# Recurrence gates as 64-row blocks, with both gates' weights side by side, in a hybrid encoder step on one core

## The chip, the core and the metric

The kernel runs on one NeuronCore of a Trainium2 chip. TensorE (PE) multiplies and PEld loads its weights; ScalarE (ACT), VectorE (DVE) and GpSimd (POOL) work beside it; SyncE (SP) issues most of the DMAs. Each engine executes its own instructions in order. The metric is the device time of one execution in microseconds (us), as a median of the runs shown.

## The reference, cut to what matters

One layer is computed for a prompt of 1024 frames and a sample of 64 frames, 1088 in all. An input projection gives, among others, the input `xa` of a recurrence with 1024 channels, a SiLU gate for it, and the operands of an attention branch. The recurrence has two sigmoid gates, `r` and `i`, whose weights are block diagonal: 16 blocks of 64 by 64.

```python
def rg_lru(u, h0, w_a, b_a, w_x, b_x, a_param):
    ub = u.reshape(B, L, N_BLOCKS_A, BLOCK_A)            # 16 blocks of 64 channels
    r = sigmoid(einsum('blnj,njk->blnk', ub, w_a).reshape(B, L, W_A) + b_a)
    i = sigmoid(einsum('blnj,njk->blnk', ub, w_x).reshape(B, L, W_A) + b_x)
    log_a = -LRU_C * r * softplus(-a_param)
    a = exp(log_a)
    x_in = sqrt(-expm1(2.0 * log_a)) * (i * u)
    # scan over time: h = a_t * h + x_t

ua, conv_new = causal_conv(xa, conv_hist, conv_w, conv_b)     # width 4
ya, h_new = rg_lru(ua, h0, w_rg_a, b_rg_a, w_rg_x, b_rg_x, a_param)
ya = ya * silu(ga)
```

The branch outputs are projected, gated, summed, projected again, normed and added to the input, and a last gated embedding is added.

## The kernel before, in words

Channels lie on partitions and time along the free dimension. The 1024 channels of the recurrence are eight groups of 128, `k` = 0 to 7, so that each group holds two of the 64-channel blocks. Every product of float32 operands is made of three matmuls: both operands are split in a high and a low part (`three`, L172 to L175, records the three lines for every such product).

The recurrence stands between the attention and the first output projection, in about 856 to 1042 us of the span. For each `k` it goes through these functions:

- `recur_in(k)` (L1456) fetches the gates' weights. It zeroes a 128x256 float32 tile `st` on POOL (L1466), and four DMAs put the four 64x64 blocks on the diagonals of its two 128x128 halves (L1471), one half for each gate. For `k` of 2 and more it returns the steps of the input projection panel of `xa`, whose three chunks of 364, 364 and 360 columns are copied out of PSUM into `xp` by ACT.
- `convolve(k)` (L1495) rounds the gate weights into `g_h` on ACT, makes the four taps of the convolution on DVE (L1501, L1504: tile `u`), and then the low part `g_l` on DVE.
- `split_u(k)` (L1509) splits `u` into `uh` (ACT) and `ul` (DVE).
- `gate(k)` (L1517) multiplies. For gate `i` (tile `x`), then for gate `r`, and for each of three chunks of 364 columns, three matmuls over 128 rows fill one bank of PSUM (`gacc`), and one ACT activation (L1526) writes 128x364 sigmoids. That makes 18 matmuls and 6 activations for each `k`.
- `mix_u`, `decay`, `decay_a`, `root`, `state_in`, `scan` and `output` (L1530 to L1586) make the recurrence on ACT and DVE: exponential, tanh and square root on ACT, the products and the scan on DVE.
- `own_gate(k)` (L1593) is the panel of the SiLU gate; its chunks are finished by ACT (L1598) and DVE (L1599). For `k` of 1, 3 and 5 it was made earlier and is only loaded; `early_gate` (L1608) finishes it.
- `split_y(k)` (L1588) splits the branch's output into `yah` and `yal`, the operands of the next projection.

Each panel's weights are loaded ahead (`look_ahead`), split by `split_next` (L284): ACT makes `wh` and a negated copy `wl`, and a DMA issued by POOL (L291) adds the raw weights onto `wl`.

The order of PE, ACT and DVE in this part is the order in which the program calls these functions (`manual_schedule`). For a pair of groups, `k` even and `k+1`, it is, on PE: gate(k), the SiLU panel of k, the input panel of k+2, gate(k+1), the input panel of k+3, and then gate(k+2). Of tiles with the suffix `_e` (odd `k`) and without it (even `k`) there is one buffer each, so that the activations of gate(k+2) write the `x` and `r` that group `k` has used. PSUM has eight banks for this part. After gate(6) PE makes the SiLU panel of 6, a third of one left-over gate panel (called f here), gate(7), the rest of f, the SiLU panel of 7 and then the first panels of the output projection (`Held`, tiles `held`), which need `yah` and `yal` one group after the other, group 7 last.

Of the kernel before, what the change touches and what calls it, by code (L numbers as in the profile page):

```python
# [8 lines left out]
F32 = mybir.dt.float32  # L9
F32R = mybir.dt.float32r  # L10
AF = mybir.ActivationFunctionType
# [3 lines left out]
P = 128  # L15
D = 1024
KT = D // P
# [6 lines left out]
HD = 64  # L24
# [13 lines left out]
W_SC = 1092  # L38
GC = 364
# [28 lines left out]
def hybrid_step(tc, a, o):  # L68
    nc = tc.nc
    PSUM = bass.MemoryType.PSUM  # L70
    act, dve, pool, pe, sp = nc.scalar, nc.vector, nc.gpsimd, nc.tensor, nc.sync

    def sb(name, bufs=1, side=None):
        kw = {"side": side} if side else {}
        return Pool(tc, name=name, bufs=bufs, reuse_waits="tile", **kw)

    def ps(name, bufs=1):
        return Pool(tc, name=name, bufs=bufs, space=PSUM, reuse_waits="tile")

    def f(ap):  # L80
        return ap.bitcast(F32)

    def copy_act(out, in_, scale=1.0):
        return act.activation(out=out, in_=in_, func=AF.Copy, scale=scale)  # L84

    def sub(eng, out, in0, in1):
        return eng.tensor_tensor(out=out, in0=in0, in1=in1, op=ALU.subtract)  # L87
# [43 lines left out]
    vt = cst.tile([P, 96], F32, name="vt")  # L131
# [4 lines left out]
    def tiny(n, name, w=1, tag=None):  # L136
        return small.tile([P, w], F32, name=name, tag=tag or name)[:n, :]
# [34 lines left out]
    def three(out, ah, al, bh, bl, start, stop):  # L172
        pe.matmul(out, ah, bh, start=start, stop=False)  # L173
        pe.matmul(out, ah, bl, start=False, stop=False)  # L174
        pe.matmul(out, al, bh, start=False, stop=stop)  # L175
# [16 lines left out]
    def panel_steps(pl, wh, wl, xs, evac, chunks=CH):  # L192

        for c, (t0, n) in enumerate(chunks):
            acc = pl.tile([P, 512], F32, name="acc", tag="acc")
            for k in range(KT):
                three(acc[:, :n], wh[:, k, :], wl[:, k, :], xs[k][0][:, t0:t0 + n], xs[k][1][:, t0:t0 + n],
                      k == 0, k == KT - 1)
                if k == KT - 1:
                    evac(c, t0, n, acc[:, :n])  # L200
                yield
# [15 lines left out]
    wpool = sb("wpool", bufs=2)  # L217
# [78 lines left out]
    def panel(eng=None, rooms=None, split=True):  # L296

        look_ahead()
        if not ahead:
            return None  # L300
        split_next(eng or dve)
        tag, _, w, *_ = ahead.popleft()
        look_ahead()
        if split:
            split_next(eng or dve, rooms)
        look_ahead()
        return tag, w
# [7 lines left out]
    mm = ps("mm", bufs=2)  # L315
# [204 lines left out]
    for name in ("conv_w", "conv_b", "b_rg_a", "b_rg_x", "a_param", "state_h", "state_conv"):  # L520
        n = a[name].shape[0]
        fetch(vec[at:at + n, :], a[name])
        at += n
    V_CW, V_CB, V_BA, V_BX, V_AP, V_H0, V_HIST = 0, 32, 40, 48, 56, 64, 72
# [67 lines left out]
    for b in range(2, NBLK + 1):  # L592
        _, n, t0 = x_src[b]
        for c, (_, w) in enumerate(VCH):
            acc = p1v.tile([P, 512], F32, name="vacc", tag="vacc")
# [700 lines left out]
    for u, (h, q2) in enumerate(units):  # L1296
        p = h // 2
# [129 lines left out]
    mm = ps("mm8", bufs=8)  # L1427
# [4 lines left out]
    def shared(n, dt, name):  # L1432
# [1 line left out]

    lent = {n: shared(n, F32, f"{n}_e") for n in ("sg", "q", "u", "e", "x", "r")}
    p3 = sb("p3")
    early = {"g": [p3.tile([P, 2, P], F32R, name=f"g_{x}") for x in "hl"], "u": p3.tile([P, W_SC], F32, name="u"),
             "uh": p3.tile([P, W_SC], F32R, name="uh"), "ul": p3.tile([P, W_SC], F32R, name="ul", tag="ul"),
             "sg": p3.tile([P, T], F32, name="sg")}
    xps, us, gws, sig, eq, states, silus, outs = {}, {}, {}, {}, {}, {}, {}, {}  # L1440
# [1 line left out]
    def cv(v, k):  # L1442
        return vt[:, v + k:v + k + 1]
# [3 lines left out]
    def room(name, k):  # L1447
        if k in lent_k:
            return lent[name][:, :]
        if name in early:  # L1450
            return early.pop(name)[:, :]
        return p3.tile([P, T if name == "sg" else W_SC], F32, name=name)[:, :]
# [3 lines left out]
    def recur_in(k):  # L1456

        if k < 2:
            xp = p3.tile([P, W_SC + 3], F32, name="xp")
            sp.dma_start(xp[:, 3:SEQ + 3], d_x[k][:, :SEQ])  # L1460
            ready_x.append(sp.dma_start(xp[:, SEQ + 6:SEQ + 6 + DEC], d_x[k][:, SEQ:T]))
            pool.memset(xp[:, 0:3], 0.0)
            pool.memset(xp[:, W_SC + 2:W_SC + 3], 0.0)
        raw = wpool.tile([P, GC], F32, name="st")[:, :2 * P].rearrange("p (i n) -> p i n", i=2)
        gh, gl = early.pop("g") if k == 0 else [p3.tile([P, 2, P], F32R, name=f"g_{x}") for x in "hl"]
        pool.memset(raw[:, :, :], 0.0)  # L1466
        for i, name in enumerate(("w_rg_a", "w_rg_x")):
            for j in range(2):
                js = slice(j * HD, (j + 1) * HD)
                with tc.issue_after(ready_x[0].ins) if k < 2 else nullcontext():  # L1470
                    sp.dma_start(raw[js, i, js], a[name][2 * k + j])  # L1471
        if k >= 2:
            xp = p3.tile([P, W_SC + 3], F32, name="xp")
            pool.memset(xp[:, 0:3], 0.0)
            pool.memset(xp[:, W_SC + 2:W_SC + 3], 0.0)
        hist = vt[:, V_HIST:V_HIST + 24].rearrange("p (j k) -> p j k", k=KT)
        pool.tensor_copy(xp[:, SEQ + 3:SEQ + 6], hist[:, :, k])

        xps[k] = xp, raw, gh, gl
        if k < 2:  # L1480
            return None

        def evac(c, t0, n, z):
            m = min(n, SEQ - t0)
            copy_act(xp[:, t0 + 3:t0 + 3 + m], z[:, :m])
            if m < n:
                copy_act(xp[:, SEQ + 6:SEQ + 6 + DEC], z[:, m:n])

        tag, w = panel()
        assert tag == ("x", k)  # L1490
        return panel_steps(mm, *w, xs, evac)
# [2 lines left out]

    def convolve(k):  # L1495
        xp, raw, gh, gl = xps.pop(k)
        copy_act(gh[:, :, :], raw[:, :, :])
        pool.tensor_copy(fin[:, 0:3, k], xp[:, SEQ:SEQ + 3])
        pool.tensor_copy(fin[:, 3:6, k], xp[:, W_SC - 1:W_SC + 2])
        u = room("u", k)  # L1500
        dve.tensor_scalar(out=u, in0=xp[:, 0:W_SC], scalar1=cv(V_CW, k), scalar2=cv(V_CB, k),  # L1501
                          op0=ALU.mult, op1=ALU.add)
        for tap in range(1, 4):
            dve.scalar_tensor_tensor(out=u, in0=xp[:, tap:tap + W_SC], scalar=cv(V_CW + tap * KT, k),  # L1504
                                     in1=u, op0=ALU.mult, op1=ALU.add)
        sub(dve, gl[:, :, :], raw[:, :, :], f(gh[:, :, :]))
        us[k], gws[k] = u, (gh, gl)

    def split_u(k):  # L1509
# [7 lines left out]
    def gate(k):  # L1517

        (u, uh, ul), (gh, gl) = us.pop(k), gws.pop(k)
        x, r = room("x", k), room("r", k)  # L1520
        for i, dst, bias in ((1, x, V_BX), (0, r, V_BA)):
            for c in range(3):
                cs_ = slice(c * GC, (c + 1) * GC)
                acc = mm.tile([P, 512], F32, name="gacc", tag="acc")
                three(acc[:, :GC], gh[:, i, :], gl[:, i, :], uh[:, cs_], ul[:, cs_], True, True)
                act.activation(out=dst[:, cs_], in_=acc[:, :GC], func=AF.Sigmoid, bias=cv(bias, k))  # L1526
        sig[k] = x, r
        mixed[k] = u

# [105 lines left out]
    seq.__enter__()  # L1635
    ga = own_gate(0)
    recur_in(0)
    convolve(0)
    recur_in(1)
    split_u(0)  # L1640
    for k in range(0, KT - 2, 2):
        ga = own_gate(k) if k else ga
        if k == 0:
            run(ga)
        gate(k)
        convolve(k + 1)
        mix_u(k)
        if k:
# [5 lines left out]
        if k:  # L1654
# [3 lines left out]
            run(ga)  # L1658
        own_gate(k + 1)
        xa = recur_in(k + 2)  # L1660
        chunk(xa)
        chunk(xa)
        if k:
            split_y(k - 1)
        run(xa)
        gate(k + 1)
        convolve(k + 2)
        mix_u(k + 1)
        decay(k)
# [14 lines left out]
    k = KT - 2  # L1684
    ga = own_gate(k)
    gate(k)
    convolve(k + 1)
    mix_u(k)
# [6 lines left out]
    tag, w = panel()  # L1695
# [71 lines left out]
    for of in range(KT):  # L1767
        g = g_ahead.popleft()
# [16 lines left out]
        else:  # L1785
            tag, w = panel()
# [93 lines left out]
    for of in range(KT):  # L1880
# [9 lines left out]
        tag, w = panel()  # L1890
# [277 lines left out]
    for k in range(2):  # L2168
        raw = p7.tile([P, D], F32, name="ple")
# [7 lines left out]
    mm = bank_pool  # L2177
# [60 lines left out]
    n = x_src[b][1]  # L2238
# [12 lines left out]
    ss, r = tiny(n, "ss"), tiny(n, "r_r")  # L2251
    dve.tensor_reduce(out=ss, in_=ss4[:n, :], axis=AX.X, op=ALU.add)
    rstd_of(ss, r, 1.0 / D)
    for i in range(2):
        c = slice(i * D // 2, (i + 1) * D // 2)
# [51 lines left out]
```

## Time and profile before

| what | value |
|---|---|
| median of 3 runs | 1441.27 us (1440.69 to 1442.69) |
| the profiled execution, its own time | 1439.48 us |
| its span, first to last instruction | 1437.7 us |
| mean granted clock of TensorE | 0.998 |
| PE busy | 1417.8 us, 99% of the span |
| DVE, ACT, POOL busy | 62%, 50%, 25% |

A row of the timeline gives the start in us, the time taken by the row's instructions together, the engine, the line, the operation, the tile that is written and those that are read, and the count. A bracket at the end tells how long the engine sat idle before it and what released it. Matmuls overlap, so that the distance between the starts of two is what one costs. A row of a group view ends with busy time, the mean of one in ns, and the idle time before.

### The profile page before, as it was taken

What the parts mean: (1) busy time and instruction counts of PE and PEld (TensorE: products, weight loads), DVE (VectorE), ACT (ScalarE), POOL (GpSimd) and SP (SyncE); (2) the same over time, 40 slices, a digit from 0 to 9 for tenths busy, and PEclk for the clock granted to TensorE, in tenths of its full rate; (3) what the DMA queues carried; (4) which work ended last, traced back from release to release, by engine and by line L of the source; (5) the groups of instructions that cost most, each with busy time, mean ns of one, the idle gap of its engine ahead of it and who ended that gap; (6) DMA issues with size and microseconds to landing.
All of it is one profiled execution on the core that took longest, in us unless ns stands there. A gap on an engine that the chain in (4) does not pass through costs nothing.

```text
span 1437.7 us, 24839 instructions
## 1 busy us (share of the span) xinstructions
PE 1417.8 (99%) x9217; PEld 1357.9 (94%) x9217; DVE 897.0 (62%) x1630; ACT 719.0 (50%) x1331; POOL 357.5 (25%) x514
## 2 busy tenths in 40 slices
PE   9999999999999999999999999999999999999997
PEld 8999999999999999999999999999999999888887
DVE  5564766564432666656666666898737574777654
ACT  5423544442213666656666657777535332665443
POOL 0013333233204545544554531321011000000001
PEclk9999999999999999999999999999999999999999
DMA  6767556864247655554474645564269773324211
GB/s 223 217 128 108 148 159 185 173 174 134 92 131 194 169 115 125 148 137 125 118 152 110 105 108 81 93 99 86 71 234 309 261 236 121 136 73 149 78 48 45
DMA packets 138917, 201.18 MB, mean 140 GB/s; under 512 B 24372, under 2 KB 98844, under 8 KB 137772
## 3 DMA queue, kind: packets, MB, share of 16 engines
q1 hardware_dynamic: 119436, 158.96, 43.5%
q0 software_dynamic: 8160, 23.25, 5.8%
q10 hardware_dynamic: 11200, 17.38, 3.3%
q8 instruction: 73, 1.20, 0.3%
q14 instruction: 48, 0.39, 0.1%
HBM read 131.60 MB, written 66.36 MB: 138 GB/s over the span
## 4 chain that ended last, share of the span: by engine, by line
PE 84%; DMA 5%; DVE 5%; ACT 3%; issue 2%; SPq 0%; DVEq 0%; ACTq 0%; POOL 0%; POOLq 0%
PE quad L820 17%; PE acc L173 11%; PE acc L175 11%; PE acc L174 11%; PE pv L1213 5%; PE q L1951 5%; PE tp L1192 4%; PE s L1171 2%; PE s L1170 2%; PE vacc L173 2%; PE vacc L174 2%; PE vacc L175 1%; DMA wl<-w_raw 1%; PE vacc L478 1%; DMA d_mix<-st_a 1%
## 5 line engine op out<-in xcount | busy, mean ns | idle before, releaser
L173 PE MATMUL acc<-xh,wh 128*128 128x364 f32 x720 | 238.1, 331 | 0.2 <-ACT st L84 0.2
L175 PE MATMUL acc<-xh,wl 128*128 128x364 f32 x720 | 235.7, 327 | 0.0
L174 PE MATMUL acc<-xl,wh 128*128 128x364 f32 x720 | 235.7, 327 | 0.0
L173 PEld LDWEIGHTS acc<-xh,wh 128*128 128x128 f32 x720 | 135.4, 188 | 1.4 <-ACT st L84 0.5
L174 PEld LDWEIGHTS acc<-xl,wh 128*128 128x128 f32 x720 | 135.3, 188 | 0.5
L175 PEld LDWEIGHTS acc<-xh,wl 128*128 128x128 f32 x720 | 135.1, 188 | 0.0
L87 DVE TENSOR_TENSOR wl<-w_raw,wh 128x1024 fp32r<-128x1024 f32 (+1 forms) x55 | 61.4, 1118 | 76.2 <-ACT wh L84 76.1
L84 ACT ACTIVATE wh<-w_raw 128x1024 fp32r<-128x1024 f32 (+1 forms) x66 | 63.4, 962 | 86.6 <-PE quad L820 34.9
L820 PE MATMUL quad<-xh,wh 128*128 128x272 f32 x416 | 87.4, 291 | 2.0 <-ACT p__3343 L84 2.0
L820 PE MATMUL quad<-xl,wh 128*128 128x272 f32 x416 | 86.1, 288 | 0.0
L820 PE MATMUL quad<-xh,wl 128*128 128x272 f32 x416 | 86.0, 288 | 0.0
L1158 POOL TENSOR_SCALAR pb<-pb,sm 128x896 f32<-128x896 f32 (+1 forms) x64 | 61.3, 957 | 88.4 <-DVE sm L1157 65.7
L87 DVE TENSOR_TENSOR tl<-tp,th 128x512 fp32r<-128x512 f32 x96 | 65.1, 685 | 27.7 <-ACT th L84 27.3
L84 ACT ACTIVATE th<-tp 128x512 fp32r<-128x512 f32 x96 | 56.7, 594 | 39.8 <-PE tp L1192 39.2
L1155 ACT ACTIVATE pb<-pb,nm 128x896 f32<-128x896 f32 (+1 forms) x64 | 63.1, 986 | 18.3 <-DVE nm L1152 14.5
L820 PEld LDWEIGHTS quad<-xh,wh 128*128 128x128 f32 x416 | 65.3, 188 | 2.5 <-ACT p__3343 L84 2.2
L1170 PE MATMUL s<-k,q 128*128 128x128 f32 (+1 forms) x192 | 66.9, 351 | 0.0
L1152 DVE CUSTOM_DVE_ANT_0 pb<-s,mask 128x896 f32<-128x896 f32 (+1 forms) x64 | 64.7, 1011 | 3.1 <-PE s L1171 3.1
L820 PEld LDWEIGHTS quad<-xh,wl 128*128 128x128 f32 x416 | 65.5, 188 | 0.0
L820 PEld LDWEIGHTS quad<-xl,wh 128*128 128x128 f32 x416 | 65.4, 188 | 0.0
L1171 PE MATMUL s<-k,q 68*128 68x128 f32 (+1 forms) x192 | 63.5, 348 | 0.8 <-DMA k<-d_k 0.8
L1192 PE MATMUL tp<-ident,pb 128*128 128x128 f32 x416 | 63.7, 273 | 0.0
(726 smaller groups left out, 4097.4 us busy)
## 6 DMA issues: line engine op xcount, KB each, us to landing
w_raw<-in_w_in SPq DMA_DIRECT2D x56, 256.0 KB
q<-d_q SPq DMA_DIRECT2D x48, 256.0 KB
k<-d_k SPq DMA_DIRECT2D x48, 256.0 KB
w_raw<-in_w_in SPq DMA_DIRECT2D x64, 128.0 KB
w_raw<-in_w_branch SPq DMA_DIRECT2D x32, 256.0 KB
wl<-w_raw POOLq DMA_DIRECT2D x11, 512.0 KB, 4.6
wraw<-in_w_in SPq DMA_DIRECT2D x20, 256.0 KB
d_k<-oh ACTq DMA_DIRECT2D x16, 272.0 KB
```

Source lines behind the costliest of these rows:

```text
L84: return act.activation(out=out, in_=in_, func=AF.Copy, scale=scale)
L87: return eng.tensor_tensor(out=out, in0=in0, in1=in1, op=ALU.subtract)
L173: pe.matmul(out, ah, bh, start=start, stop=False)
L174: pe.matmul(out, ah, bl, start=False, stop=False)
L175: pe.matmul(out, al, bh, start=False, stop=stop)
L820: pe.matmul(acc[:, c, :CW], l[:, k, :], r[:, k, c * CW:(c + 1) * CW], start=(first and k == 0 and p == 0), stop=(k == 3 and p == 2), skip_ ...
L1152: at = book("D", now[0] + HOP_PE, per(D_MAX, n), lambda: dve.tensor_tensor_reduce(out=pr[:, :n], in0=s[:, :n], in1=m, scale=-1.0, scalar=- ...
L1170: pe.matmul(s[:, c0:c0 + w], t["q1"][:, q0:q0 + P], t["k1"][:, c0:c0 + w], start=True, stop=False)
L1171: pe.matmul(s[:, c0:c0 + w], t["q2"][:HD + 4, q0:q0 + P], t["k2"][:HD + 4, c0:c0 + w], start=False, stop=True)
L1192: pe.transpose(tp[:, o0 + i * P:o0 + (i + 1) * P], pr[par][:, kb * P:(kb + 1) * P], ident[:, :])
L1213: return pe.matmul(pv[:, c0:256], v, x[:, half * 256 + c0:(half + 1) * 256], **kw)
L1951: pe.matmul(acc, l[:, k, :], r[:, k, :], start=(first and k == 0 and i == 0), stop=(k == 3 and i == 2), skip_group_check=not first)
```

## The change

Each 64-row block is multiplied on its own. The stationary operand of a block is 64 rows by 128 columns and holds both gates' weights side by side; the block in the lower 64 partitions (j = 0) has the `i` gate's weights in the first 64 columns and the `r` gate's in the last 64, the block in the upper 64 partitions (j = 1) the other way round. The two blocks have a bank of PSUM each, and their matmuls take turns. A bank then holds both gates of one block: one gate's on the partitions where it belongs, the `r` gate's on the other 64. So each bank is finished by two activations of 64 partitions, of which the one for `r` writes to the other half of the partitions. Its bias comes from a small tile `b_ra` in which the halves of the bias are exchanged.

The matmuls stay 18 for each `k`, each with 64 rows instead of 128; the activations become 12 of 64x364 instead of 6 of 128x364. Tiles `g_h`, `g_l` and the raw weights are 128 columns wide instead of 256, the memset of `st` goes, and the four DMAs of 64x64 stay.

```diff
+    b_ra = p3.tile([P, KT], F32, name="b_ra")
+    for j in range(2):
+        pool.tensor_copy(b_ra[(1 - j) * HD:(2 - j) * HD, :], vt[j * HD:(j + 1) * HD, V_BA:V_BA + KT])
-    early = {"g": [p3.tile([P, 2, P], F32R, name=f"g_{x}") for x in "hl"], ...
+    early = {"g": [p3.tile([P, P], F32R, name=f"g_{x}") for x in "hl"], ...
...
-        raw = wpool.tile([P, GC], F32, name="st")[:, :2 * P].rearrange("p (i n) -> p i n", i=2)
-        pool.memset(raw[:, :, :], 0.0)
+        raw = wpool.tile([P, GC], F32, name="st")[:, :P]
...
-                    sp.dma_start(raw[js, i, js], a[name][2 * k + j])
+                    c0 = HD * (i == j)
+                    sp.dma_start(raw[js, c0:c0 + HD], a[name][2 * k + j])
...
-        for i, dst, bias in ((1, x, V_BX), (0, r, V_BA)):
-            for c in range(3):
-                cs_ = slice(c * GC, (c + 1) * GC)
-                acc = mm.tile([P, 512], F32, name="gacc", tag="acc")
-                three(acc[:, :GC], gh[:, i, :], gl[:, i, :], uh[:, cs_], ul[:, cs_], True, True)
-                act.activation(out=dst[:, cs_], in_=acc[:, :GC], func=AF.Sigmoid, bias=cv(bias, k))
+        blocks = [slice(j * HD, (j + 1) * HD) for j in range(2)]
+        for c in range(3):
+            cs_ = slice(c * GC, (c + 1) * GC)
+            accs = [mm.tile([P, 512], F32, name="gacc", tag="acc") for _ in blocks]
+            for i, (g, v) in enumerate(((gh, uh), (gh, ul), (gl, uh))):
+                for js, acc in zip(blocks, accs):
+                    pe.matmul(acc[:, :GC], g[js, :], v[js, cs_], start=(i == 0), stop=(i == 2))
+            for js, other, acc in zip(blocks, blocks[::-1], accs):
+                act.activation(out=x[js, cs_], in_=acc[js, :GC], func=AF.Sigmoid, bias=vt[js, V_BX + k:V_BX + k + 1])
+                act.activation(out=r[js, cs_], in_=acc[other, :GC], func=AF.Sigmoid, bias=b_ra[other, k:k + 1])
```

More of the change, by code (lines that the diff above doesn't have):

```diff
@@ L1436, in hybrid_step @@
     p3 = sb("p3")
-    early = {"g": [p3.tile([P, 2, P], F32R, name=f"g_{x}") for x in "hl"], "u": p3.tile([P, W_SC], F32, name="u"),
+    b_ra = p3.tile([P, KT], F32, name="b_ra")
+    for j in range(2):
+        pool.tensor_copy(b_ra[(1 - j) * HD:(2 - j) * HD, :], vt[j * HD:(j + 1) * HD, V_BA:V_BA + KT])
+    early = {"g": [p3.tile([P, P], F32R, name=f"g_{x}") for x in "hl"], "u": p3.tile([P, W_SC], F32, name="u"),
              "uh": p3.tile([P, W_SC], F32R, name="uh"), "ul": p3.tile([P, W_SC], F32R, name="ul", tag="ul"),
@@ L1463, in recur_in @@
             pool.memset(xp[:, W_SC + 2:W_SC + 3], 0.0)
-        raw = wpool.tile([P, GC], F32, name="st")[:, :2 * P].rearrange("p (i n) -> p i n", i=2)
-        gh, gl = early.pop("g") if k == 0 else [p3.tile([P, 2, P], F32R, name=f"g_{x}") for x in "hl"]
-        pool.memset(raw[:, :, :], 0.0)
+        raw = wpool.tile([P, GC], F32, name="st")[:, :P]
+        gh, gl = early.pop("g") if k == 0 else [p3.tile([P, P], F32R, name=f"g_{x}") for x in "hl"]
         for i, name in enumerate(("w_rg_a", "w_rg_x")):
@@ L1496, in convolve @@
         xp, raw, gh, gl = xps.pop(k)
-        copy_act(gh[:, :, :], raw[:, :, :])
+        copy_act(gh[:, :], raw)
         pool.tensor_copy(fin[:, 0:3, k], xp[:, SEQ:SEQ + 3])
@@ L1505, in convolve @@
                                      in1=u, op0=ALU.mult, op1=ALU.add)
-        sub(dve, gl[:, :, :], raw[:, :, :], f(gh[:, :, :]))
+        sub(dve, gl[:, :], raw, f(gh[:, :]))
         us[k], gws[k] = u, (gh, gl)
```

## The prediction

> **What bounds the kernel now.** I read the page first, then the waits of PE around the recurrence, then the timelines of the engines there, ACT's beside DVE's.
>
> ```profile
> span 1437.7 us, 24839 instructions
> PE 1417.8 (99%) x9217; PEld 1357.9 (94%) x9217; DVE 897.0 (62%) x1630; ACT 719.0 (50%) x1331; POOL 357.5 (25%) x514
> ```
>
> ```profile
> PE pv L1213 <- DVE y L1239: 0.6, 1, 0.6
> PE pv L1213 <- DVE diag0l L87: 0.3, 1, 0.3
> PE held L173 <- DVE st_a L1774: 0.2, 1, 0.2
> PE acc L173 <- ACT st L84: 0.2, 1, 0.2
> ```
>
> PE is busy all the time. The four rows of the second view are all its waits between 830 and 1080 us: 1.3 us. By these alone the kernel is bound by PE and every matmul that goes is a gain. But a share of busy time doesn't say how far PE is from its next wait, so the next rows look at its order in the recurrence: the first matmul of gates 1, 2, 4, 6, of the left-over panel f, of gate 7, and of what follows it.
>
> ```profile
> 881.18 0.33 PE L173 MATMUL gacc<-uh,g_h 128*128 128x364 f32 x1
> ...
> 896.10 0.33 PE L173 MATMUL gacc<-uh,g_h 128*128 128x364 f32 x1
> ...
> 937.85 0.33 PE L173 MATMUL gacc<-uh,g_h 128*128 128x364 f32 x1
> ...
> 979.60 0.33 PE L173 MATMUL gacc<-uh,g_h 128*128 128x364 f32 x1
> ...
> 994.51 0.33 PE L173 MATMUL acc<-xh,wh 128*128 128x364 f32 x1
> ...
> 998.51 0.33 PE L173 MATMUL gacc<-uh,g_h 128*128 128x364 f32 x1
> ...
> 1001.84 0.43 PE L173 MATMUL acc<-xh,wh 128*128 128x364 f32 x1 [0.17 <-ACT st L84]
> ```
>
> From gate 2 to gate 4, and again from 4 to 6, PE needs 41.75 us: three panels of 72 matmuls and two gates of 18, which are 252, so 0.166 us each. Now ACT over the same pair of groups:
>
> ```profile
> 881.38 0.53 ACT L84 ACTIVATE xp<-acc 128x296 f32<-128x296 f32 x2 [3.53 <-PE acc L175]
> 881.88 1.57 ACT L1526 ACTIVATE x_e<-gacc,vt 128x364 f32<-128x364 f32 x3
> ...
> 884.85 0.41 ACT L84 ACTIVATE g_h<-st 128x256 fp32r<-128x256 f32 x1
> ...
> 903.00 1.47 ACT L1526 ACTIVATE x<-gacc,vt 128x364 f32<-128x364 f32 x3 [0.47 <-DVE e L1567]
> ...
> 913.27 0.47 ACT L1598 ACTIVATE sg<-acc 128x364 f32<-128x364 f32 x1 [5.12 <-DVE yal L87]
> ...
> 923.15 1.11 ACT L84 ACTIVATE yah<-r_e 128x1088 fp32r<-128x1088 f32 x1 [3.55 <-DVE r_e L1586]
> ...
> 924.56 1.48 ACT L1526 ACTIVATE x_e<-gacc,vt 128x364 f32<-128x364 f32 x3
> 925.90 1.50 ACT L1526 ACTIVATE r_e<-gacc,vt 128x364 f32<-128x364 f32 x3
> 927.24 0.46 ACT L84 ACTIVATE g_h<-st 128x256 fp32r<-128x256 f32 x1
> ...
> 938.89 1.12 ACT L1556 ACTIVATE r<-r 128x1092 f32<-128x1092 f32 x1
> ...
> 945.45 1.02 ACT L1526 ACTIVATE x<-gacc,vt 128x364 f32<-128x364 f32 x2 [0.47 <-DVE e L1567]
> ...
> 987.91 1.48 ACT L1526 ACTIVATE x<-gacc,vt 128x364 f32<-128x364 f32 x3 [0.48 <-DVE e L1567]
> ```
>
> The activations of gates 2, 4 and 6 start 42.45 and 42.46 us apart, each released by the scan of two groups before (L1567 on DVE), not by PE, whose gate 2 was under way at 896.10. So beside PE's round of 41.75 us there runs a second one of 42.45 us, on ACT and DVE alone: scan, DVE's work up to 923.15, ACT's from there without a pause to the square root at 938.89, DVE's again up to the next scan. PE is carried by the lead that it has. How large that still is, DVE shows where it makes the operand `ul` of gates 4, 6 and 7 (third, fifth and sixth row):
>
> ```profile
> 911.89 1.28 DVE L87 TENSOR_TENSOR yal<-sg,yah 128x1088 fp32r<-128x1088 f32 x1
> ...
> 924.29 1.29 DVE L87 TENSOR_TENSOR yal<-r_e,yah 128x1088 fp32r<-128x1088 f32 x1 [0.74 <-ACT yah L84]
> ...
> 934.55 1.30 DVE L87 TENSOR_TENSOR ul<-u,uh 128x1092 fp32r<-128x1092 f32 x1 [2.49 <-ACT uh L84]
> ...
> 940.04 1.30 DVE L1560 SCALAR_TENSOR_TENSOR r<-e,r 128x1092 f32<-128x1092 f32 x1
> ...
> 977.00 1.30 DVE L87 TENSOR_TENSOR ul<-u,uh 128x1092 fp32r<-128x1092 f32 x1 [2.49 <-ACT uh L84]
> ...
> 995.60 1.29 DVE L87 TENSOR_TENSOR ul<-u_e,uh 128x1092 fp32r<-128x1092 f32 x1
> ```
>
> `ul` of group 4 is there at 935.85 and PE takes it at 937.85: 2.0 us to spare. For group 6 it is 978.30 and 979.60: 1.3 us. For group 7, 996.89 and 998.51: 1.6 us. Whatever makes the ACT-DVE round longer reaches PE after that, and a faster PE only arrives earlier at the same wait. The weights are as close: the low part of a panel's weights is a DMA that POOL issues behind ACT's split and, for f, behind two copies that wait for the scan.
>
> ```profile
> 976.26 0.87 POOL L291 DMA_DIRECT2D wl<-w_raw  x1 [2.91 <-ACT wl L84]
> ...
> 989.19 0.90 POOL L291 DMA_DIRECT2D wl<-w_raw  x1
> ```
>
> ```profile
> wl<-w_raw POOLq DMA_DIRECT2D x11, 512.0 KB, 4.6
> ```
>
> With the 4.6 us of the DMA view (median from issue to landing), the panel after gate 6 has its weights at 980.9 and f at 993.8, 0.7 us before its first matmul at 994.51.
>
> **The matmuls.** Nothing in this trace has 64 rows in each half of the array by turns. The nearest rows are the scores, with 68 rows and with 128:
>
> ```profile
> L1170 PE MATMUL s<-k,q 128*128 128x512 f32 x96 | 40.0, 417 | 0.0
> ...
> L1171 PE MATMUL s<-k,q 68*128 68x512 f32 x96 | 38.1, 397 | 0.0
> ```
>
> Half the rows leave a matmul as long as before, so the gain depends on whether the two blocks run at once. If they do, a pair costs one step of 0.166 us and a gate 9 steps, 1.5 us less; if not, 18 steps and nothing saved. I take the former, since the two blocks share neither rows, operands nor a bank, and keep both ends: at most 12 us of PE over eight gates. The Trainium skill (TensorE: Matmul & The Clock Gate, Part 3, measured speedup) gives 3.07 times for four blocks of 32 rows; an estimate by it, at the same efficiency for two (1.54 times), is 1.05 us a gate, and no run here shows it yet.
>
> **The activations.** Six more for each group. What 64 partitions cost against 128, both from PSUM, 256 columns:
>
> ```profile
> L84 ACT ACTIVATE lo<-pv 64x256 f32<-64x256 f32 x64 | 24.4, 381 | 26.8 <-PE pv L1213 21.2 <-PE pv L1279 1.5 <-DVE ys L1285 1.4
> ...
> L84 ACT ACTIVATE st<-tpk 128x256 f32<-128x256 f32 x19 | 6.9, 378 | 6.8 <-DMA out_k_prompt<-st 6.8
> ```
>
> 381 against 378 ns: half the partitions save nothing, and `lo` even moves partitions as the new `r` does. Three sigmoids go from 924.56 to 925.90, 0.447 us each. Twelve take 5.36 us, six 2.68, so each gate costs ACT 2.68 us more. Over eight gates that is 21 us, but only those on the round count:
>
> - Even gates, at 903.00: ACT later waits 5.12 us for DVE. The added 2.68 us delay `yah`, which `yal` at 911.89 needs; ACT has it there about 0.9 us early even so. Nothing, unless the activations are 0.1 us longer than I take them.
> - Odd gates, at 924.56: ACT doesn't pause from there to the square root (ending at 940.01, just ahead of DVE's `r` at 940.04). All 2.68 us go into the round. Further, `r_e` is now written second, at 925.01, while DVE reads the old `r_e` in `yal` from 924.29 to 925.58: a wait of 0.6 us, behind which the other activations queue. The narrower `g_h` (0.46 us) gives back between nothing and half; I take 0.1. Sum 3.2 us for each of gates 3 and 5.
> - Gate 1: ACT waits for PE (3.53 us), so PE's gain counts. PE starts 1.5 us earlier, at 879.68; the first activation came 0.70 us after gate 1 began (three steps and 0.2), so now at 880.38, and twelve end at 885.74, where `g_h` started at 884.85. With the 0.1 back: 0.8 us later.
>
> So the round is 0.8 us late after gate 1, 4.0 after gate 3 and 7.2 after gate 5. Then PE: `ul` of group 6 is there at 985.5, gate 6 ends at 987.0; its panel's weights land at 988.1 and it needs 11.9 us (982.6 to 994.51), so it ends at 1000.0; the weights of f land at 993.8 + 7.2 = 1001.0; a third of f (4.0 us) ends at 1005.0, when `ul` of group 7 (1004.1) is there; gate 7 ends at 1006.5. Before, what follows started at 1001.84: 4.7 us later. All 12 us saved on PE are in front of these waits and are lost there, except 1.5 at gate 7, already counted.
>
> Edits at nothing: eight memsets fewer and two small copies more on POOL (busy 25%); the copies' cover is the first SiLU panel. DMAs stay as many and as large. From 1001.84 on PE's next tie to the round is `yal` of group 7:
>
> ```profile
> 1041.10 1.29 DVE L87 TENSOR_TENSOR yal<-r,yah 128x1088 fp32r<-128x1088 f32 x1
> ```
>
> ```profile
> 1049.81 0.34 PE L173 MATMUL held<-yah,wh 128*128 128x364 f32 x1
> ```
>
> There at 1042.39 and taken at 1049.81, it stays off the path with the round 7.2 and PE 4.7 us later, so the delay stays to the end. On the profiled execution's 1439.48 us this makes 1444.2; on the median of 1441.27, 1.8 above it, **1446.0 us**.
>
> **Rivals.**
> - *The two blocks don't overlap*, so that the change doesn't do what it says. Gate 1 then gives its first bank after six steps instead of three, at 882.38, and ACT is 2.8 us late after it; 9.2 after gate 5. Gate 6 from 987.5 to 990.5, its panel to 1002.4, weights of f at 1003.0, gate 7 from 1007.0 to 1010.0: 8.2 us, so 1449.5. For it: no row shows an overlap. Against: nothing shared.
> - *Faster: the activations of 64 partitions are short, so that the round doesn't grow.* By the sums above PE's delay is the round's delay less 2.5 us (7.2 against 4.7), and the round's delay is 36 times one activation (twelve after each of gates 1, 3 and 5) less 8.9 us. Break-even is at 0.32 us an activation. At half of 0.447, in proportion to the partitions, the round gains 0.9 us and PE 3.4: 1437.9. (With no round to wait for it would be the whole 12 us: 1429.3.) Against it: 381 and 378 ns.
> - *No change*: activations between, near 0.32 us, or an ACT pause that I have overlooked takes them up: 1441.3.
> - PE idles for over 4 us ahead of gates 4 and 6 in my forecast. The Trainium skill (TensorE: Matmul & The Clock Gate, Part 1) says that idling of some 3.4 us halves TensorE's clock until about as long a stretch of work has passed. By that rule, an estimate, the restart after the last such wait costs up to 1.7 us, and the time would be 1447.7. No wait here is that long, so the trace is silent.
>
> **How the numbers follow.** The forecast has 0.55, the halves in turn without overlap 0.20, the faster rival 0.12, no change 0.13. The forecast's own range is 1444.2 (0.40 us an activation) to 1447.8 (0.50), which are 36 times 0.05 us up or down. The range over the cases leaves out the faster rival and little above the serial one: 1441 to 1450. About 0.2%, 2.9 us, is what a measurement of this kernel can tell from no change. Slower by more holds the forecast and the serial case, 0.75; same 0.13; faster 0.12.
>
> **What would show it.** Right: matmuls of `gacc` starting in pairs a few ns apart; 96 activations of 64x364 about 0.45 us apart; the activations of gate 6 at about 995.1 instead of 987.91; new waits of PE for `ul` of groups 4 and 6; what follows gate 7 at about 1006.5; fewer us of PE busy, in a longer span. Wrong: PE without new waits in the recurrence, activations much under 0.4 us apart, or gate 6 on ACT no later than before.

## The result, and the profile after

The changed kernel takes **1455.69 us** (median of five runs, 1453.88 to 1457.43) against 1441.27: a ratio of 1.01, 95% interval 1.0087 to 1.0113. It is slower, by 14.4 us. Of five executions of the kernel before, four took 1440.18 to 1442.69 us and one, which no comparison here counts, 2315.88. The forecast had the sign and the mechanism; its 1446.0 is a third of the way, and the range ended at 1450. The profiled execution took 1453.88 us, 14.4 more than the one before.

The page of the changed kernel:

```profile
span 1452.0 us, 24893 instructions
PE 1416.9 (98%) x9217; PEld 1350.4 (93%) x9217; DVE 895.9 (62%) x1630; ACT 749.5 (52%) x1379; POOL 355.9 (25%) x508
```

PE has nearly the same busy time in a span that is 14.3 us longer. Counted over the recurrence alone (window; length, then busy time and instructions of PE, PEld, DVE, ACT and POOL, then granted clock of TensorE (1.00 is full speed), DMA share and rate), first before, then after:

```profile
860.00:1020.00 160.00, 159.83 (x964) 159.52 (x964) 128.36 (x133) 117.82 (x169) 30.77 (x63) 1.00 0.51 90
```

```profile
860.00:1035.00 175.00, 159.08 (x965) 152.29 (x964) 126.03 (x129) 145.36 (x214) 28.09 (x57) 0.96 0.46 82
```

The same matmuls take 15 us longer here. PE went from no pause to 16 us of pauses, and ACT has 27.5 us more to do, in 45 instructions more. PE's waits between 830 and 1080 us, which were 1.3 us in all, are now led by these:

```profile
PE gacc L1530 <- ACT uh L84: 7.5, 3, 3.3
PE acc L173 <- DVE sg L1606: 3.1, 2, 2.1
PE gacc L1530 <- DVE ul L87: 2.7, 3, 0.9
PE acc L173 <- ACT st L84: 1.3, 1, 1.3
```

The gates wait for both halves of `u`, which ACT and DVE make late in their round. **The matmuls** did what the change says. Gate 0 on PE after (before it took from 866.26 to 869.27):

```profile
866.63 0.44 PE L1530 MATMUL gacc<-uh,g_h 64*128 64x364 f32 x2
866.90 0.33 PE L1530 MATMUL gacc<-ul,g_h 64*128 64x364 f32 x2
867.07 0.33 PE L1530 MATMUL gacc<-uh,g_l 64*128 64x364 f32 x2
...
868.09 0.33 PE L1530 MATMUL gacc<-uh,g_l 64*128 64x364 f32 x2
868.35 0.44 PE L173 MATMUL acc<-xh,wh 128*128 128x364 f32 x1
```

Each row is a pair, one block in the upper rows and one in the lower. The pairs follow each other at 0.166 us, as single matmuls did: the two blocks run at once. Only the step into the short form (866.63 to 866.90) and the one out of it (868.09 to 868.35) are 0.1 us longer. A gate takes 1.72 us instead of 3.01.

**The activations** are another matter. Those of gate 3 on ACT, after:

```profile
928.80 0.55 ACT L1532 ACTIVATE x_e<-gacc,vt 64x364 f32<-64x364 f32 x1
929.85 0.56 ACT L1533 ACTIVATE r_e<-gacc,b_ra 64x364 f32<-64x364 f32 x1 [0.50 <-DVE yal L87]
930.44 0.56 ACT L1532 ACTIVATE x_e<-gacc,vt 64x364 f32<-64x364 f32 x1
931.01 0.56 ACT L1533 ACTIVATE r_e<-gacc,b_ra 64x364 f32<-64x364 f32 x1
...
935.60 0.56 ACT L1533 ACTIVATE r_e<-gacc,b_ra 64x364 f32<-64x364 f32 x1
936.19 0.31 ACT L84 ACTIVATE g_h<-st 128x128 fp32r<-128x128 f32 x1
```

From 929.85 to 936.19 eleven activations take 6.34 us: they start 0.576 us apart, as on the other gates, where the forecast had 0.447. One alone lasts no longer than before (the 128-partition ones have medians of 564 to 590 ns). What has gone is that one started before the last had ended. The predicted wait of `r_e` for the old `yal` is there, 0.50 us instead of 0.6.

How late the round is can be read at the first activation of each gate. Before, gates 2, 4, 6 and 7 started at 903.00, 945.45, 987.91 and 1004.95. After:

```profile
906.23 0.56 ACT L1532 ACTIVATE x<-gacc,vt 64x364 f32<-64x364 f32 x1 [0.47 <-DVE e L1574]
...
954.22 0.56 ACT L1532 ACTIVATE x<-gacc,vt 64x364 f32<-64x364 f32 x1 [0.47 <-DVE e L1574]
...
1002.19 0.56 ACT L1532 ACTIVATE x<-gacc,vt 64x364 f32<-64x364 f32 x1 [0.43 <-DVE e L1574]
...
1016.59 0.46 ACT L84 ACTIVATE st<-acc 128x364 f32<-128x364 f32 x1
...
1020.22 0.56 ACT L1532 ACTIVATE x_e<-gacc,vt 64x364 f32<-64x364 f32 x1 [1.64 <-DVE e_e L1574]
```

That is 3.23, 8.77, 14.28 and 15.27 us late. With the odd gates between them (924.56 became 928.80, 967.01 became 976.79) the delay grows by 3.23 us over gate 1, by 1.01 over gate 2, 4.53 over gate 3, 1.01 over gate 4, 4.50 over gate 5 and 0.99 over gate 6. PE's first matmul behind gate 7 moves from 1001.84 to 1017.10, 15.26 us, and the first `held` from 1021.84 to 1037.01, 15.17. From there to the end about 0.8 us come back; single executions scatter by more than that.

So gates 3 and 5 cost 4.5 us each instead of 3.2, gate 1 costs 3.2 instead of 0.8, and an even gate, forecast as covered, costs 1.0. Where that cover failed shows on DVE, in the rows of group 2. Before:

```profile
905.09 4.14 DVE L1504 SCALAR_TENSOR_TENSOR u_e<-xp,vt,u_e 128x1092 f32<-128x1092 f32 x3
909.15 0.42 DVE L87 TENSOR_TENSOR g_l<-st,g_h 128x256 fp32r<-128x256 f32 x1
```

After:

```profile
908.32 4.14 DVE L1507 SCALAR_TENSOR_TENSOR u_e<-xp,vt,u_e 128x1092 f32<-128x1092 f32 x3
913.51 0.29 DVE L87 TENSOR_TENSOR g_l<-st,g_h 128x128 fp32r<-128x128 f32 x1 [1.05 <-ACT g_h L84]
```

`g_l` needs `g_h`, which ACT makes behind the last activation. Before, `g_h` was there at 906.14 (905.69 and 0.45) and DVE came for it at 909.15, 3.0 us to spare. Twelve activations at 0.576 are 4.2 us longer than six at 0.447; with 0.14 back for the narrower `g_h`, the spare time is overdrawn by 1.1 us, and DVE waits 1.05. The forecast looked one step too far on, at `yah` for `yal`.

### The profile page after: what moved, and what is told of

It reads as the page before. It is cut to its first block, busy times and chain, and to the rows that moved or that the text cites. A ratio compares the mean times of both kernels' runs of the same rounds, so it can differ in the third digit from the quotient of the medians.

```text
span 1452.0 us, 24893 instructions
## 1 busy us (share of the span) xinstructions
PE 1416.9 (98%) x9217; PEld 1350.4 (93%) x9217; DVE 895.9 (62%) x1630; ACT 749.5 (52%) x1379; POOL 355.9 (25%) x508
## 4 chain that ended last, share of the span: by engine, by line
PE 84%; DMA 5%; DVE 5%; ACT 4%; issue 2%; SPq 0%; POOL 0%; DVEq 0%; ACTq 0%; POOLq 0%
PE quad L820 17%; PE acc L173 11%; PE acc L175 11%; PE acc L174 11%; PE pv L1213 5%; PE tp L1192 4%; PE q L1958 4%; PE s L1171 2%; PE s L1170 2%; PE vacc L173 2%; PE vacc L174 1%; PE vacc L175 1%; PE vacc L478 1%; DMA d_mix<-st_a 1%; DMA d_q<-ko 1%
```

## Experiments

The theory after the result: the time goes into ACT's round, and what was mis-sized is the pace of the activations, with 0.13 us more for each. Its rivals: the 64-row matmuls themselves cost something; PE's own time counts, so that any saving there must show; the pace comes from the 64 partitions as such, or from writing to other partitions than are read; and TensorE's clock, which falls in the new waits, is part of the bill.

**1. New matmuls, six activations.** In the changed kernel each bank is finished by one activation over all 128 partitions, as before.

```diff
-            for js, other, acc in zip(blocks, blocks[::-1], accs):
-                act.activation(out=x[js, cs_], in_=acc[js, :GC], ...)
-                act.activation(out=r[js, cs_], in_=acc[other, :GC], ...)
+            for dst, v, acc in zip((x, r), (V_BX, V_BA), accs):
+                act.activation(out=dst[:, cs_], in_=acc[:, :GC], func=AF.Sigmoid, bias=cv(v, k))
```

> The changed kernel's 64-row matmuls, but each bank of PSUM is finished by one activation of 128 partitions, six for each group as in the kernel before. The gates come out wrong: half of each activation takes the other gate's values. Theory A (the twelve activations lengthen the ACT-DVE round, and TensorE's gain can't be had because it waits for the round): activations 0.45 us apart, no long wait of PE, and about 1438.5 us, so 3 us under the kernel before (1441.3) and far less than the 10 us that eight gates of 1.72 instead of 3.01 us save on PE. Theory B (the 64-row matmuls themselves, or the exchange between the array's two ways of working, cost the time): 1450 us or more. Theory C (nothing but PE counts): 1431.

Measured: 1440.7 us, ratio to before 1.0005 (0.9995 to 1.0015). No change: the 64-row matmuls cost nothing, and PE's shorter gates bring nothing either. Gate 3 on ACT:

```profile
923.49 0.57 ACT L1532 ACTIVATE x_e<-gacc,vt 128x364 f32<-128x364 f32 x1
924.60 0.57 ACT L1532 ACTIVATE r_e<-gacc,vt 128x364 f32<-128x364 f32 x1 [0.55 <-DVE yal L87]
925.06 0.56 ACT L1532 ACTIVATE x_e<-gacc,vt 128x364 f32<-128x364 f32 x1
925.51 0.56 ACT L1532 ACTIVATE r_e<-gacc,vt 128x364 f32<-128x364 f32 x1
```

The pace is 0.45 us again. I had expected about 3 us of gain. The round did start earlier (gate 2 at 902.06, 0.94 us; gate 3 at 923.49, 1.07 us), but in the new order `r_e` is written second and waits 0.55 us for `yal`; the same at gate 5. At gate 6 there are 0.13 us left. On PE the saving has turned into pauses:

```profile
860.00:1020.00 160.00, 154.12 (x969) 147.62 (x968) 128.06 (x133) 116.77 (x169) 34.44 (x57) 1.00 0.51 90
```

It idles 5.9 us of 160 where it had idled 0.2.

**2. Old matmuls, twelve activations.** The counterpart: 18 matmuls of 128 rows as before, and the twelve activations in the changed kernel's order. The edit is shown against the changed kernel; the wide weight tiles of the kernel before are back too.

```diff
-            for i, (g, v) in enumerate(((gh, uh), (gh, ul), (gl, uh))):
-                for js, acc in zip(blocks, accs):
-                    pe.matmul(acc[:, :GC], g[js, :], v[js, cs_], ...)
+            for i, acc in zip((1, 0), accs):
+                three(acc[:, :GC], gh[:, i, :], gl[:, i, :], uh[:, cs_], ul[:, cs_], True, True)
```

> The kernel before's 128-row matmuls, but finished by the twelve activations of 64 partitions of the changed kernel, in their order. The r gate is wrong: its halves are taken from the other half's channels. Theory A: the round is as long as in the changed kernel, gate 1's first activation is 1.1 us later (it waits for six steps of PE) and gate 7 takes 1.3 us longer: about 1458 us. Theory B (the matmuls cost the time): 1441 to 1444.

Measured: 1456.94 us in its one execution, so without an interval. Its activations start 0.58 us apart, and gate 6 is 16.5 us late:

```profile
1004.40 0.56 ACT L1528 ACTIVATE x<-gacc,vt 64x364 f32<-64x364 f32 x1 [0.48 <-DVE e L1570]
```

With before, after and the first experiment this fills the four fields: six activations take about 1441 us with either kind of matmul, twelve take 1456 to 1457 with either. The loss lies in the activations.

**3. What sets their pace.** Old matmuls, and in each group the bank is finished by another form, all else equal: 64 partitions in place or crossed over, lower and upper half by turns or grouped, half the columns, all of it twice.

```diff
+                if k == 0:
+                    for h in (lo, up):
+                        sigm(*held[-1], h, h)
...
+        if k in (1, 3):
+            for h, o_ in ((lo, up), (up, lo)):
+                for e_ in held:
+                    sigm(*e_, h, h if k == 1 else o_)
```

> The kernel before's matmuls; each group finishes its gates in another way, so that one trace shows what an activation of each form takes from start to start. Group 0: lower then upper 64 partitions of each bank, in place. 1: all lower halves of the six banks, then all upper. 2: as 0, but written to the other 64 partitions. 3: as 1, but written to the other 64 partitions. 4: 128 partitions, 182 columns, twice. 5: the changed kernel's pattern. 6: 128 partitions and 364 columns, twice the same. 7: as before. Some gates come out wrong in groups 2, 3 and 5 (taken from other channels). Theory P (activations in which the 64 partitions change from one to the next don't overlap at their ends): 0.57 us in groups 0, 2 and 5, 0.45 within the runs of groups 1 and 3, 0.45 in 6 and 7. Theory X (writing to other partitions than are read prevents it): 0.57 in 2, 3 and 5 and 0.45 in 0 and 1. Theory H (any 64-partition activation does): 0.57 in 0, 1, 2, 3 and 5. Group 4: about 0.30.

Group 0, in place, by turns (x2: two activations in a row of the view), from one pair to the next 1.15 us:

```profile
869.85 1.13 ACT L1525 ACTIVATE x<-gacc,vt 64x364 f32<-64x364 f32 x2
871.01 1.14 ACT L1525 ACTIVATE r<-gacc,vt 64x364 f32<-64x364 f32 x2
872.16 1.14 ACT L1525 ACTIVATE x<-gacc,vt 64x364 f32<-64x364 f32 x2
```

Group 3, crossed, grouped; the half changes once, after 934.71:

```profile
933.36 0.55 ACT L1525 ACTIVATE x_e<-gacc,vt 64x364 f32<-64x364 f32 x1
933.81 0.55 ACT L1525 ACTIVATE r_e<-gacc,vt 64x364 f32<-64x364 f32 x1
934.26 0.55 ACT L1525 ACTIVATE x_e<-gacc,vt 64x364 f32<-64x364 f32 x1
934.71 0.56 ACT L1525 ACTIVATE r_e<-gacc,vt 64x364 f32<-64x364 f32 x1
935.28 0.56 ACT L1525 ACTIVATE x_e<-gacc,vt 64x364 f32<-64x364 f32 x1
935.74 0.55 ACT L1525 ACTIVATE r_e<-gacc,vt 64x364 f32<-64x364 f32 x1
```

In a run on the same half they start 0.45 us apart; where the half changes, 0.57 (934.71 to 935.28). Crossing costs nothing (in place and grouped: 0.45 too; crossed by turns: 0.58), and neither do 64 partitions as such. The changed kernel's own pattern, in group 5, came to 0.576, there with the two activations of a pair on different banks, so that reading one bank twice isn't the cause. In these groups an activation starts before the one ahead has ended, by some 0.12 us, except when it reads or writes other partitions than that one did; and in the changed kernel one of the two changes every time (`x` reads and writes the first 64, `r` reads the other 64 and writes the first, the next `x` reads and writes the other 64). Half the columns for all partitions, 128x182 twice, were 0.295 us each, so that splitting by columns would also have cost 0.14 us a bank. One form came out otherwise than expected: 128x364 twice from the same bank took about 1.05 us a pair. The starts, 1003.43, 1004.03, 1004.50 and 1005.08, show that the second of a pair waits for the end of the first (0.60 and 0.58 us) and that the next pair follows 0.47 us later. The two of a pair write the same elements, while the half columns, which also read one bank twice but write different elements, start about 0.30 us apart within a pair and between pairs. That the repeated writing is the reason was not tested further.

The Trainium skill (ScalarE: Activation LUTs, "What ACT_TABLE_LOAD costs") gives 280 ns and 0.833 ns a column for an activation with a bias from memory, and an overlap of 93 ns back to back. By that page 364 columns are 583 ns, and 490 from start to start; the trace has 561 and 447 on one set of partitions and 576 when it changes, so an overlap like the page's is seen only in the first case, with 114 ns.

**4. The waits filled.** The clock rule of the prediction's last rival can now be seen. After the waits of 3.3 and 0.9 us ahead of gate 4, the granted clock (last column but two) is 0.50 for 6.4 us:

```profile
944.60:951.00 6.40, 6.32 (x28) 5.92 (x29) 6.19 (x9) 6.33 (x7) 0.00 (x0) 0.50 0.75 111
951.00:955.00 4.00, 4.00 (x26) 4.00 (x25) 3.90 (x4) 3.47 (x8) 3.27 (x3) 0.99 0.46 51
```

The same follows the wait ahead of gate 6. The experiment keeps PE busy there with matmuls into a bank that nobody reads.

```diff
+        if k in (4, 6):
+            spare = mm.tile([P, 512], F32, name="spare", tag="acc")
+            for i in range(24):
+                pe.matmul(spare[:, :GC], xs[0][0][:, :P], xs[1][0][:, :GC], start=(i == 0), stop=(i == 23))
```

> The changed kernel, with 24 matmuls on operands long at hand, into a bank that nobody reads, put ahead of gates 4 and 6 where PE waits for its operand. They are 4.0 us at full clock, as long as the waits (3.3 and 0.9 us each). Theory A with the clock: the waits let the granted clock fall to 0.5 for about 6 us (matmuls 0.30 us apart behind gates 4 and 6); filled, the clock stays at 1, the round is the same, and about 2.5 us come back at gate 6: 1453. Theory D (the clock's fall is hidden by the round): the same time as the changed kernel, 1455.7.

```profile
943.90:951.00 7.10, 6.32 (x43) 5.54 (x42) 6.88 (x9) 7.03 (x7) 0.00 (x0) 1.00 0.78 119
```

The clock stays at 1.00, and the time doesn't fall: 1456.98 us, ratio to before 1.0117 (1.01 to 1.0134) against 1.01 (1.0087 to 1.0113) for the changed kernel, the first `held` at 1037.09 against 1037.01. The Trainium skill (TensorE: Matmul & The Clock Gate, Part 1) has the clock halved after an idle window of about 3.4 us and full again after at least one busy window of that length. The trace agrees on the fall, after waits of 3.33 and 0.90 us; the half speed lasted 6.4 us. Yet the half-speed stretch, about 3 us of lost matmuls, is not on the path: what PE loses in it, it would otherwise spend waiting for ACT and DVE (with the clock held, its waits for `sg` grew from 3.1 to 4.2 us). My expectation that this would give some time back fell.

**5. The same activations, grouped.** The cure that the third experiment suggests: all three `x` and three `r` of one block, then those of the other, so that the partitions change three times a gate instead of eleven.

```diff
+            held.append((cs_, accs))
+        for j, (js, other) in enumerate(zip(blocks, blocks[::-1])):
+            for cs_, accs in held:
+                act.activation(out=x[js, cs_], in_=accs[j][js, :GC], ...)
+            for cs_, accs in held:
+                act.activation(out=r[js, cs_], in_=accs[j][other, :GC], ...)
```

> The changed kernel, its twelve activations in another order: for the block in the lower partitions the three chunks of x and then the three of r, then the same for the upper block, so that the partitions read and written change three times within a group instead of at every activation. Theory P (a change of partitions costs an activation 0.12 us, the rest 0.45): first activation to g_h 8 times 0.45 and 4 times 0.57, 5.9 us instead of 6.9; the wait of r_e for the old yal (0.5 us) goes; even gates are covered again; the round is late by 2.3 after gate 1 and 3.0 more at each of gates 3 and 5, 8.3 us in all: about 1449.5. Rival (64 partitions or the count of activations cost, not their order): as the changed kernel, 1455.7.

Measured: 1447.83 us, ratio to before 1.0049 (1.0034 to 1.0065), 7.9 us better than the changed kernel and 6 slower than before. Gate 2 and then DVE's `g_l`:

```profile
906.25 1.46 ACT L1535 ACTIVATE x<-gacc,vt 64x364 f32<-64x364 f32 x3 [0.47 <-DVE e L1579]
907.72 1.47 ACT L1538 ACTIVATE r<-gacc,b_ra 64x364 f32<-64x364 f32 x3
909.21 1.46 ACT L1535 ACTIVATE x<-gacc,vt 64x364 f32<-64x364 f32 x3
910.69 1.46 ACT L1538 ACTIVATE r<-gacc,b_ra 64x364 f32<-64x364 f32 x3
912.17 0.31 ACT L84 ACTIVATE g_h<-st 128x128 fp32r<-128x128 f32 x1
```

```profile
912.51 0.29 DVE L87 TENSOR_TENSOR g_l<-st,g_h 128x128 fp32r<-128x128 f32 x1
```

Twelve activations take 5.9 us, `g_h` is there just in time, and `g_l` has no wait: the even gates are covered again (gate 3 is 3.26 us late, as gate 2 was 3.25). The odd ones cost 3.05 us each. That is the forecast's picture with its own price of an activation, but the first `held` is 9.31 us late, not 4.7. Of the 4.6 us between, 2.5 are the other error, PE's supposed lead, and 2.4 come from gate 1, after which the round is 3.25 us late instead of 0.8; gates 3 and 5 take 0.15 us each less than the 3.2. Of gate 1's part 1.26 us are a late start of this execution: it began gate 0 that much later (867.52 against 866.26), and 1.11 of it were there at the first `pv` matmul of the attention, long before the recurrence (467.26 against 466.15).

**6 and 7. The change in the even groups only, and in the odd groups only.** The other groups keep the old form; the second kernel has (1, 3, 5, 7).

```diff
+    BLOCKWISE = (0, 2, 4, 6)
...
+        if k in BLOCKWISE:
+            blocks = [slice(j * HD, (j + 1) * HD) for j in range(2)]
...
+        for i, dst, bias in () if k in BLOCKWISE else ((1, x, V_BX), (0, r, V_BA)):
...
```

> The change made in groups 0, 2, 4 and 6 alone; the odd ones are as before. If only the activations of odd gates lie on the round, and those of even ones are covered up to 0.9 us by ACT's wait for DVE: gate 1 starts 0.6 earlier, each of gates 2, 4 and 6 adds 1.0, 2.4 us in all: about 1443.5. Rival (every gate's six added activations cost the same): half of the change's loss, 1448.5.

> The change made in groups 1, 3, 5 and 7 alone. If only odd gates lie on the round: 3.9 us at gate 1, 4.5 at each of gates 3 and 5, 12.9 us in all: about 1454. Rival (every gate the same): 1448.5.

Even groups: 1443.18 us, ratio 1.0016 (1.0007 to 1.0025). Odd groups: 1453.74, ratio 1.0087 (1.0071 to 1.0103). If every gate cost the same, both would stand near 1448.5; that falls. With the even groups changed, gates 2, 4 and 6 put 1.25, 1.24 and 1.5 us into the round, most of it as a wait of DVE for `g_h`; gate 2's:

```profile
909.41 0.42 DVE L87 TENSOR_TENSOR g_l<-st,g_h 128x256 fp32r<-128x256 f32 x1 [1.15 <-ACT g_h L84]
```

With the odd ones changed, gates 3 and 5 cost 4.6 us each and the even gates nothing. The first `held` is 2.80 and 14.8 us late. Together that is more than the 15.2 of the whole change, but the second execution was behind from long before: its first `pv` matmul starts at 467.93 us instead of 466.15, and gate 0 on PE at 868.09 instead of 866.26. Counted from each execution's own gate 0, the first `held` is 2.5 and 12.9 us late, and 14.8 with the whole change; the medians are 1.7, 12.2 and 14.4 us above those before. By either count the two make up about the whole.

**8. Group 0 only, grouped.** Gate 0 is the one gate that is off the round: its activations, ahead of the first scan, have slack, and its shorter matmuls let PE reach gate 1 sooner.

```diff
+    BLOCKWISE = (0,)
```

> The change made in group 0 alone, with the grouped order of activations: there ACT has idle time until PE brings the next panel, and the start of the round waits for PE, so that 1.3 us less on PE should start the round about 0.6 to 0.9 us earlier, and nothing should become longer: 1440.0, 0.05% under the kernel before, at the edge of what can be measured. If PE's gain is worth something wherever it is made: 1.3 us. If the exchange between 64-row and 128-row matmuls costs: the time of before or above.

Measured: 1439.48 us, ratio to before 0.9984 (0.9975 to 0.9992): faster than both kernels, by less than the 0.2% that I took as measurable from one set of runs. In the trace gate 6 on ACT is at 987.43 instead of 987.91 and the first `held` at 1021.36 instead of 1021.84, 0.48 us earlier. This execution was behind, too, when it came to gate 0 (866.96 against 866.26; 0.61 us of it were there at the first `pv` matmul), so that from gate 0 on it gains 1.18 us, about what PE saves in that gate. The interval, 1.2 to 3.6 us, begins there; the rest of the 2 us between the medians the trace doesn't explain.

## Why the prediction was right, and where it failed

- **What bounds the kernel:** right. The two rounds of 41.75 and 42.45 us, 0.7 us apart, decide: experiment 1 makes PE's shorter and gains nothing, experiment 2 makes ACT's longer and loses as much as the whole change.
- **The matmuls:** right. The blocks overlap; a gate saves 1.29 us, not 1.5, for the steps into and out of the short form; the estimate by the Trainium skill (TensorE: Matmul & The Clock Gate, Part 3), 1.05 us, was too low. The rival without overlap falls.
- **The activations: the failed step.** "Three sigmoids go from 924.56 to 925.90, 0.447 us each. Twelve take 5.36 us, six 2.68". A start-to-start distance of one form was taken for the price of another. That 64 partitions last as long as 128 was right, but part of the 0.447 was the overlap with the neighbour, and the change's order of partitions takes that away: 0.576. On gates 1, 3 and 5 this is 36 times 0.129, 4.6 us.
- **Even gates:** "Nothing, unless the activations are 0.1 us longer than I take them." They were, by 0.13, and each cost 1.0 us, 3.0 in all. The cover was also read at the wrong place: `g_l` waiting for `g_h` binds before `yal`, with 3.0 us of cover for the whole addition. (At `yal` the 0.9 us left were 1.06 by the rows: `yah` ended at 908.15, `yal` began at 911.89, less 2.68.)
- **Odd gates:** the wait for `yal` and the narrower `g_h` as forecast (0.50 and 0.15 us); 4.5 instead of 3.2 by the pace.
- **Gate 1:** its first activation was taken at 880.38 and came at 881.26. PE started gate 0 0.37 us later than before (866.63 against 866.26; 0.22 of it were there at the first `pv` matmul), gate 0 and the panels behind it saved 1.09 us together instead of 1.5 (gate 1 at 880.46), and the first bank took 0.80 us, 0.1 more. That is 0.9 us.
- **PE's lead:** "PE's delay is the round's delay less 2.5 us". It wasn't: 15.27 on ACT, 15.26 on PE. The row that shows it was quoted, and only its start was used: what follows gate 7 began at 1001.84 with a wait of 0.17 us for ACT's `st`. PE had 1.6 us to spare at `ul` of gate 7 and nothing three microseconds later. After the change the same wait is there, with 1.35 us:

```profile
1017.10 0.43 PE L173 MATMUL acc<-xh,wh 128*128 128x364 f32 x1 [1.35 <-ACT st L84]
```

The forecast's 4.7 us, with 4.6 for the pace on the odd gates, 3.0 for the even ones, 2.5 for the lead and 0.9 for gate 1, make 15.7 against 15.2 seen; gates 3 and 5 came out 0.2 us each below this sum. Experiment 5 separates the first two errors from the others: near the price that the forecast used (0.49 us on the average), the delay is 9.3 us, of which 1.3 are that execution's own late start.

- **The rivals:** that short activations make it faster falls with 0.55 to 0.57 us each. The clock falls, as that rival has it, but that costs nothing which experiment 4 could show: what PE loses at half speed it would otherwise wait for ACT and DVE.
- **The range** took the unknown cost as 0.40 to 0.50 us an activation, though the rows at hand gave a wider bound: three activations took 1.48 us while starting 0.447 us apart, so that one alone is 1.48 less 0.89, 0.59 us. As the upper end that is 36 times 0.14 us more, 5 us, and with the even gates uncovered by some 1.2 us each the range would have ended near 1455.

## What to carry to other kernels

An engine that is 99% busy may still only be keeping step with a loop of other engines; measure both rounds between the same two points, and before giving an engine a lead, look at every wait up to the end, also the one of 0.2 us. Splitting an evacuation (the copying of results out of PSUM) by partitions bought nothing on ScalarE here, since 64 partitions took as long as 128, and it doubles the instructions; if it must be, order them so that consecutive ones stay on the same partitions. Price an instruction between its start-to-start distance and its own length, and take the far end when its neighbours change.

## What the runs showed of the hardware

- Consecutive activations of 364 columns on the same partitions start 0.45 us apart though each lasts 0.56; when the 64 partitions read or written change, 0.58.
- Two 64-row matmuls of 364 columns in the two halves of the array cost one step, 0.166 us; going from 128 rows to 64 and back costs 0.1 us each time.
- After a wait of 3.3 and 0.9 us with one pair between, TensorE's granted clock was 0.50 for about 6.4 us.
